# Layer B's first eight gate blocks as four block pairs ahead of the queries, gates kept in DRAM, scores and row minimum in one operation

## The chip, the cores and the metric

The kernel runs on one core of a Trainium2 chip. The metric is the device time of one execution in microseconds (us). TensorE (PE) multiplies matrices, VectorE (DVE) and ScalarE (ACT) work element by element, GpSimd (POOL) does some element work and issues transfers that add into their target, and SyncE (SP) issues nearly all other transfers, one after the other from one queue: a transfer that has to wait holds back all that stand behind it.

## The reference, cut to what matters

One step of a two-layer decoder on 576 tokens (512 of a prompt, 64 of eight samples), width 2048. Layer A is gated linear attention. Then one shared K and V is computed, and layer B is sliding-window attention with 32 heads, a sink per head and a distance penalty. Layer B is what the change touches:

```python
kv = rmsnorm(h, g_norm_kv) @ w_kv                   # shared K and V, 4 heads of 64
q, z = split(rmsnorm(h, g_norm_b) @ w_in, 2)        # w_in 2048 x 4096: 2048 columns q, 2048 columns z
s = (q . k) * HD ** -0.5 - slope * dist             # per head; -inf where not allowed
m = max(max(s), sink)
p = exp(s - m);  denom = sum(p) + exp(sink - m)
o = (p / denom) @ v
h = h + (o * silu(z)) @ w_out                       # silu(z): the gate
y = rmsnorm(h, g_final)
```

k and v of the last rows are outputs as well (`k_win_*`, `v_win_*`).

## The kernel before, in words

Activations lie with channels on the 128 partitions and the 576 tokens along the row. A weight matrix is taken in blocks of 128 output columns. Every fp32 product is done as three products of split numbers (high by high, high by low, low by high): a 512-wide piece of a weight block is loaded as `raw` (SP, L174), ACT rounds it to `wh` (L169), DVE subtracts to get `wl` (L170).

A **dense block** (`dense`) has 16 row tiles x 3 products x 2 token halves = 96 matmuls of 128 x 288 (L181). A **block pair** (`dense_pair`, used so far in the two output projections) computes two blocks with seven half-size products named A, P4, P5, B, P6, P7, C in that order, each of 8 row tiles x 3 = 24 matmuls (L251): 168 instead of 192. It needs sums of activations: `t1` in the second half of the x tiles, and `t2`, `t3`, `t4`, built by `sums` (L263, L267, L268) from the residual tiles `hp`. It also needs sums of weight quarters: the tiles `rs`, which SP loads (L231) and onto which a POOL transfer adds a second quarter from DRAM (L233). P5 uses the first such tile (`s1`), P7 the second (`s3`); the pair's plain quarters `w11`, `w22`, `w12` are `raw` tiles. Each stage opens its own memory pool over the space of the stage before, so its first tiles wait until all users of the old ones are done.

Layer B runs in this order. Four dense blocks for K and V, with the norm gain of K and V folded into the split of x. Keys are written to DRAM (`dk`, L928, L929), V stays in the tile `vm`; the window outputs are stored (L951 to L955). x is split again with layer B's gain (L96, L97). Then come 16 dense blocks q0 to q15 and 16 dense blocks z0 to z15. The attention runs as a background generator beside them: for each of 64 units (a head pair and 128 queries) and 16 sample units it inserts its few matmuls between those of the dense blocks. A unit of the prompt forms `slope*dist - score` with two DVE operations (L1028), takes the minimum with one (L1031), and goes on with exp, sum, reciprocal, scaling, transposes and the product with V. A sample unit does the same with three operations (L1092 twice, L1095) and one minimum (L1098). When a z block ends, its gate silu(z) is formed and multiplied onto the attention's result (L887 to L891); the background must have reached that head group by then.

The last six z blocks run in the pool of the output stage, with `sums` beside them; then follow one dense block of the output projection, six pairs and the last three blocks.

Of the kernel before, what the change touches and what calls it, by code (L numbers as in the profile page):

```python
# [37 lines left out]
def kernel(ctx: ExitStack, tc: tile.TileContext, A, O):  # L38
# [840 lines left out]

    units_done = [0]  # L880

    def z_phase(js):
        def ev(j):
            def f(p):
# [7 lines left out]
                if j < 8:  # L892
                    dma(dg2[j], hpt(j)[:, HT:NT])
            return f
        for j in js:
            yield from dense(A["wB"], KT + j, ev(j))

    with tc.tile_pool(name="ap", bufs=1) as ap:
# [13 lines left out]
        kw = ap.tile([128, 2, 256], F32, name="kw", tag="s", bufs=3)  # L912

        for k in range(KT):
            split_gain(k, hpt(k), GKV)

        def ev_k(m):
            def f(p):
                if m == 0:
                    finish(make_rstd(ssB[0], D, rstd, (0, 1)))  # L920
                t = st()
                vec.tensor_tensor(halves(t), p, rB2, ALU.mult)
                kh = ap.tile([128, NT], F32R, tag="stE", name=nm("kh"), bufs=2)
                kl = ap.tile([128, NT], F32R, tag="stO", name=nm("kl"), bufs=2)
                nc.scalar.copy(kh, t)
                vec.tensor_tensor(kl, t, f32(kh), ALU.subtract)
                for u in range(2):
                    dma(dk[2 * m + u, 0], f32(kh[u * 64:(u + 1) * 64, :]))  # L928
                    dma(dk[2 * m + u, 1], f32(kl[u * 64:(u + 1) * 64, :]))  # L929
                pt = bank(m)  # L930
                for i, c0 in enumerate((384, 448)):
                    nc.tensor.transpose(out=pt[:, i * 128:(i + 1) * 128], in_=t[:, c0:c0 + 128], identity=ident)
                nc.scalar.copy(kw[:, :, m * 128:(m + 1) * 128], pt[:, 0:256].rearrange("p (i f) -> p i f", i=2))
            return f

        def ev_v(m):
            def f(p):
                t = st()
                vec.tensor_tensor(halves(t), p, rB2, ALU.mult)
                pt = bank(2 + m)  # L940
                pt2 = bank(m)
                for i, c0 in enumerate((0, 128, 256, 384)):
                    nc.tensor.transpose(out=pt[:, i * 128:(i + 1) * 128], in_=t[:, c0:c0 + 128], identity=ident)
                nc.tensor.transpose(out=pt2[:, 0:128], in_=t[:, 448:576], identity=ident)
                nc.scalar.copy(vm[:, 0:4, m * 128:(m + 1) * 128], pt.rearrange("p (i f) -> p i f", i=4))
                nc.scalar.copy(vm[:, 4, m * 128:(m + 1) * 128], pt2[:, 0:128])
            return f

        run(chain(dense(A["wKV"], 0, ev_k(0)), dense(A["wKV"], 1, ev_k(1)),
                  dense(A["wKV"], 2, ev_v(0)), dense(A["wKV"], 3, ev_v(1))))  # L950
        dma(O["k_win_prompt"], kw[:, 0, :])  # L951
        dma(O["v_win_prompt"], vm[:, 3, :])
        for i in range(8):
            dma(O["k_win_sample"][i, 120:128], kw[64 + 8 * i:72 + 8 * i, 1, :])
            dma(O["v_win_sample"][i, 120:128], vm[64 + 8 * i:72 + 8 * i, 4, :])  # L955
        dma(O["k_win_sample"][:, 0:120], A["cache_k"][:, 8:128])
# [379 lines left out]
```

## Time and profile before

| | us |
|---|---|
| median of three runs | 1756.82 |
| the three runs | 1755.49, 1756.82, 1758.81 |
| the profiled execution | 1759.1 |
| its span in the profile | 1757.3 |
| PE busy in the span | 1728.8 |
| DVE busy | 1296.8 |
| ACT busy | 853.0 |

The profile is one execution. Its rows give start and duration of instructions or groups of them; a row of waits names the engine and line that waited and the one whose event ended the wait. The median lies 2.3 us below the profiled execution.

### The profile page before, as it was taken

What the parts mean: (1) busy time and instruction counts of PE and PEld (TensorE: products, weight loads), DVE (VectorE), ACT (ScalarE), POOL (GpSimd) and SP (SyncE); (2) the same over time, 40 slices, a digit from 0 to 9 for tenths busy, and PEclk for the clock granted to TensorE, in tenths of its full rate; (3) what the DMA queues carried; (4) which work ended last, traced back from release to release, by engine and by line L of the source; (5) the groups of instructions that cost most, each with busy time, mean ns of one, the idle gap of its engine ahead of it and who ended that gap; (6) DMA issues with size and microseconds to landing.
All of it is one profiled execution on the core that took longest, in us unless ns stands there. A gap on an engine that the chain in (4) does not pass through costs nothing.

```text
span 1757.3 us, 33753 instructions
## 1 busy us (share of the span) xinstructions
PE 1728.8 (98%) x12846; PEld 1709.1 (97%) x12846; DVE 1296.8 (74%) x2799; ACT 853.0 (49%) x1771; POOL 135.8 (8%) x216
## 2 busy tenths in 40 slices
PE   7999999999999999999999999999999999999996
PEld 7999999999999999999999999999999999999996
DVE  8566776777777777658777866888879885587784
ACT  7533334434434444435444655766666653364451
POOL 3000001001001000100111100100100000002210
PEclk9999999999999999999999999999999999999998
DMA  8246643565465444532677543343333225226643
GB/s 300 98 151 190 194 156 112 160 197 166 134 195 174 123 138 151 153 101 87 189 219 209 162 133 97 106 119 101 106 88 109 89 76 169 81 95 195 195 149 108
DMA packets 126690, 253.84 MB, mean 144 GB/s; under 512 B 22944, under 2 KB 52512, under 8 KB 126496
## 3 DMA queue, kind: packets, MB, share of 16 engines
q1 hardware_dynamic: 122784, 238.05, 42.2%
q0 software_dynamic: 3744, 13.63, 4.3%
q8 instruction: 101, 1.65, 0.4%
q14 instruction: 61, 0.50, 0.1%
HBM read 196.19 MB, written 44.83 MB: 137 GB/s over the span
## 4 chain that ended last, share of the span: by engine, by line
PE 91%; DVE 3%; issue 3%; DMA 2%; ACT 1%; SPq 0%; POOL 0%; POOLq 0%; DVEq 0%; ACTq 0%
PE pd L181 60%; PE pb L251 15%; PE pb L629 2%; PE pb L1041 1%; PE pb L715 1%; PE pb L1024 1%; PE pb L804 1%; PE pb L803 1%; PE pb L801 1%; PE pb L1023 1%; DVE wl L170 1%; PE pb L716 1%; PE pb L1051 1%; PE pb L1052 1%; DVE x L97 1%
## 5 line engine op out<-in xcount | busy, mean ns | idle before, releaser
L181 PE MATMUL pd<-x,wh 128*128 128x288 f32 x5568 | 1017.7, 299 | 10.1 <-ACT x L96 6.9
L181 PEld LDWEIGHTS pd<-x,wh 128*128 128x128 f32 x5568 | 837.0, 189 | 18.0 <-ACT x L96 6.9
L181 PE MATMUL pd<-x,wl 128*128 128x288 f32 x2784 | 614.1, 298 | 1.1 <-DVE wl L170 0.9
L169 ACT CAST wh<-raw 128x512 fp32r<-128x512 f32 x426 | 263.1, 618 | 403.7 <-PE pd L181 327.0
L181 PEld LDWEIGHTS pd<-x,wl 128*128 128x128 f32 x2784 | 454.1, 189 | 4.5 <-DVE wl L170 1.8
L170 DVE TENSOR_TENSOR wl<-raw,wh 128x512 fp32r<-128x512 f32 x426 | 306.2, 720 | 143.3 <-ACT wh L169 138.9
L251 PE MATMUL pb<-x,wh 128*128 128x288 f32 x832 | 166.7, 295 | 0.0
L251 PEld LDWEIGHTS pb<-x,wh 128*128 128x128 f32 x832 | 133.4, 188 | 0.0
L251 PE MATMUL pb<-t,wh 128*128 128x288 f32 x624 | 125.8, 296 | 0.7 <-ACT wh L169 0.6
L251 PE MATMUL pb<-x,wl 128*128 128x288 f32 x416 | 122.2, 295 | 0.0
L170 DVE TENSOR_TENSOR wl<-rs,wh 128x512 fp32r<-128x512 f32 x104 | 82.1, 793 | 32.2 <-ACT wh L169 30.0
L169 ACT CAST wh<-rs 128x512 fp32r<-128x512 f32 x104 | 64.0, 620 | 83.6 <-PE pb L251 76.6
L251 PEld LDWEIGHTS pb<-t,wh 128*128 128x128 f32 x624 | 100.2, 188 | 1.1 <-ACT wh L169 0.9
L251 PE MATMUL pb<-t,wl 128*128 128x288 f32 x312 | 92.4, 297 | 0.4 <-DVE wl L170 0.4
L251 PEld LDWEIGHTS pb<-x,wl 128*128 128x128 f32 x416 | 78.0, 188 | 0.0
L119 POOL TENSOR_TENSOR acc<-acc,st 128x576 f32<-128x576 f32 x46 | 70.1, 1523 | 83.1 <-ACT st L114 82.2
L117 POOL COPY acc<-st 128x576 f32<-128x576 f32 x7 | 6.3, 906 | 863.9 <-ACT st L114 775.9
L783 ACT CAST sh<-Si 128x512 fp32r<-128x512 f32 x64 | 39.7, 620 | 66.4 <-PE pb L803 43.6
L1033 ACT ACTIVATE s<-s,tiny 128x257 f32<-128x257 f32 (+1 forms) x128 | 60.9, 478 | 21.1 <-DVE tiny L1031 20.8
L114 ACT ACTIVATE st<-hp 128x576 f32<-128x576 f32 (+1 forms) x66 | 43.3, 663 | 40.8 <-DVE hp L1203 21.8
L251 PEld LDWEIGHTS pb<-t,wl 128*128 128x128 f32 x312 | 58.7, 188 | 0.8 <-DVE wl L170 0.8
L805 DVE SCALAR_TENSOR_TENSOR Si<-Si,dl,pb 128x512 f32<-128x512 f32 x64 | 47.5, 742 | 12.3 <-PE pb L801 11.7
(265 smaller groups left out, 2370.3 us busy)
## 6 DMA issues: line engine op xcount, KB each, us to landing
raw<-in_wA_dram SPq DMA_DIRECT2D x92, 512.0 KB
raw<-in_wB_dram SPq DMA_DIRECT2D x64, 512.0 KB
Si<-in_state_dram SPq DMA_DIRECT2D x64, 256.0 KB
out_gla_sample_dram<-Si SPq DMA_DIRECT2D x64, 256.0 KB
raw<-in_wOB_dram SPq DMA_DIRECT2D x26, 512.0 KB
raw<-in_wOA_dram SPq DMA_DIRECT2D x25, 512.0 KB
rs<-in_wOA_dram SPq DMA_DIRECT2D x14, 512.0 KB
rs<-in_wOA_dram POOLq DMA_DIRECT2D x14, 512.0 KB, 8.6
```

What stands on the lines that cost most here:

```text
L97: vec.scalar_tensor_tensor(t[:, 1, :], src, g, f32(t[:, 0, :]), ALU.mult, ALU.subtract)
L114: act(sq[:, lo:hi], src, AF.Square)
L119: self.eng.tensor_tensor(self.acc[:, lo:hi], self.acc[:, lo:hi], sq[:, lo:hi], ALU.add)
L169: nc.scalar.copy(wh, raw)
L170: vec.tensor_tensor(wl, raw, f32(wh), ALU.subtract)
L181: mm(p[:, a, :HT], w, x[:, part, a * HT:(a + 1) * HT], start=(k == 0 and w is wh and part == 0), stop=(k == KT - 1 and w is wl))
L251: mm(p, wt[:, kk, :], xpart(x, k, part), start=(opens and k == 0 and wt is wh and part == 0), stop=(k == 7 and wt is wl), skip_group_check ...
L629: mm(p[:, o:o + N], keys(li)[:, f * 128:(f + 1) * 128], queries(li)[:, f, :], start=(f == 0), stop=(f == 1))
L715: mm(p[:, sl], S[:, f, sl], qe[:, f, :], start=(f == 0), stop=False)
L783: nc.scalar.copy(sh, Si)
L805: vec.scalar_tensor_tensor(Si, Si, dl[:, f * 16 + i:f * 16 + i + 1], p, ALU.mult, ALU.add)
L1033: act(s[:, e, off:257], s[:, e, off:257], AF.Exp, scale=-1.0, bias=tiny[:, e:e + 1], accum_out=tiny[:, 2 + e:3 + e])
```

## The change

During the K/V blocks the residual `hp` is scaled in place by layer B's gain, and `sums_of_h` builds `t2`, `t3`, `t4` from it in the background. After the K/V blocks `vm` is stored to DRAM (`dvm`) and its pool is released; a new pool over that space holds the weight sums `rs` and two gate tiles. Four block pairs compute the z blocks 0 to 7; their gates go to DRAM (`dz`). Then the second halves of x are restored and the attention's pool opens, with `vm` loaded back. The z phase that is left covers blocks 8 to 15; each of its evictions also multiplies a stored gate onto block j - 8. In the attention, q is divided by minus the slope, so that one operation forms (score + dist) times slope and the minimum with the sink.

```diff
+    def pair_z(j):
+        def silu(j, rs):
+            th = st()
+            act(th, rs, AF.Tanh)
+            vec.scalar_tensor_tensor(rs, th, 1.0, rs, ALU.add, ALU.mult)
+            dma(dz[j], rs)
+        def f(n, p):
...
+            elif n == "P7":
+                vec.tensor_tensor(halves(r1), halves(r1), p.unsqueeze(1).broadcast_to([128, 2, HT]), ALU.subtract)
+                vec.scalar_tensor_tensor(r1, r1, 0.5, rstd, ALU.mult, ALU.mult)
+                silu(j + 1, r1)
+            elif n == "C":
+                vec.tensor_tensor(r0[:, HT:NT], p, u, ALU.subtract)
+                vec.scalar_tensor_tensor(r0[:, HT:NT], r0[:, HT:NT], 0.5, rstd[:, HT:NT], ALU.mult, ALU.mult)
+                silu(j, r0)
...
     def z_phase(js):
...
                 vec.tensor_tensor(hpt(j), hpt(j), rs, ALU.mult)
-                if j < 8:
-                    dma(dg2[j], hpt(j)[:, HT:NT])
+                i = j - 8
+                vec.tensor_tensor(hpt(i), hpt(i), early, ALU.mult)
+                dma(dg2[i], hpt(i)[:, HT:NT])
+            early = tpool[0].tile([128, NT], F32, tag="ld", name=nm("ld"), bufs=2)
+            dma(early, dz[j - 8])
...
+            def sums_of_h():
+                for g in range(4):
+                    for k in (2 * g, 2 * g + 1, 2 * g + 8, 2 * g + 9):
+                        act(hpt(k), hpt(k), AF.Copy, scale=vecs[:, GB + k:GB + k + 1])
+                        yield
+                    yield from sums_hp(g)
+            bgs.append([sums_of_h(), 1.1, 0.0])
...
+            dma(dvm, vm)
+            drain()
+        with tc.tile_pool(name="zq", bufs=1) as zq:
+            tpool[0] = zq
...
+            for j in range(0, 8, 2):
+                run(dense_pair(A["wB"], KT + j, pair_z(j)))
+    for k in range(8):
+        split_half(k, hpt(k)[:, HT:NT])
...
-            for e in range(2):
-                vec.scalar_tensor_tensor(s[:, e, off:256], distp[:, off:256], slope(2 * m + e),
-                                         p[:, e * 256 + off:(e + 1) * 256], ALU.mult, ALU.subtract)
-            tiny = tiny_tile()
-            vec.tensor_reduce(tiny[:, 0:2], s[:, :, off:257], AX.X, ALU.min)
+            tiny = tiny_tile()
+            for e in range(2):
+                i = 2 * m + e
+                vec.tensor_tensor_reduce(s[:, e, off:256], p[:, e * 256 + off:(e + 1) * 256], distp[:, off:256],
+                                         slope(i), sinkp[:, i:i + 1], ALU.add, ALU.min, tiny[:, e:e + 1])
...
-        run(z_phase(range(RS)))
+        run(z_phase(range(8, RS)))
```

The sample units are changed in the same way (three of the new operations each).

The first place is SP's queue behind the last K/V block. Before, the stores of `vm` (`out_v_win_*`) are followed by weights for the next q blocks (`raw`):

```order
L174 DMA raw_1712_12131<-in_wB_dram 128x1024
L174 DMA raw_1713_12133<-in_wB_dram 128x1024
L174 DMA raw_1749_12357<-in_wB_dram 128x1024
L952 DMA out_v_win_prompt_dram<-vm_11352 128x256
L955 DMA out_v_win_sample_dram<-vm_11352 8x256 x8
L174 DMA raw_1750_12359<-in_wB_dram 128x1024
L174 DMA raw_1785_12612<-in_wB_dram 128x1024
L976 DMA stE_1707_12120<-qh_1709_12122 64x576
```

In the changed kernel `raw_1707` and `raw_1709` are w22 and w12 of the first pair, `raw_1749` is w11 of the second, `rs_1708` and `rs_1710` are s1 and s3 of the first, `rs_1751` is s1 of the second:

```order
L231 DMA raw_1707_12084<-in_wB_dram 128x1024
L231 DMA raw_1709_12089<-in_wB_dram 128x1024
L231 DMA raw_1749_12346<-in_wB_dram 128x1024
L996 DMA out_v_win_prompt_dram<-vm_11345 128x256
L999 DMA out_v_win_sample_dram<-vm_11345 8x256 x8
L1003 DMA dvm_11338<-vm_11345 128x1280
L231 DMA rs_1708_12086<-in_wB_dram 128x1024
L231 DMA rs_1710_12091<-in_wB_dram 128x1024
L231 DMA rs_1751_12350<-in_wB_dram 128x1024
```

Behind the stores of `vm` there now stands the store `dvm`, and behind that the load of `rs_1708`, whose tile lies on the space that `vm` leaves.

The second place is TensorE at the same point. Before, the transposes of the last V block (`st` to `pb3` and `pb1`, L943, L944) stand inside block q0:

```order
L181 MATMUL pd_1695_12001<-x5_1684_11968,wh_1700_12034 128x288 x4
L181 MATMUL pd_1695_12001<-x5_1684_11968,wl_1701_12035 128x288
L943 MATMUL pb3_1677_11924<-c_ident_131,st_1676_11922 128x128 x4
L944 MATMUL pb1_1678_11925<-c_ident_131,st_1676_11922 128x128
L181 MATMUL pd_1695_12001<-x5_1684_11968,wl_1701_12035 128x288
L181 MATMUL pd_1695_12001<-x6_1685_11971,wh_1700_12034 128x288 x4
```

In the changed kernel they stand between product A (the last matmul of which is the first row here) and product P4:

```order
L251 MATMUL pb0_1711_12094<-x7_1697_12053,wl_1715_12112 128x288
L978 MATMUL pb3_1684_11976<-c_ident_131,st_1683_11974 128x128 x4
L979 MATMUL pb1_1685_11977<-c_ident_131,st_1683_11974 128x128
L251 MATMUL pb1_1719_12131<-t4_1631_11514,wh_1720_12132 128x288 x2
L251 MATMUL pb1_1719_12131<-t4_1631_11514,wl_1721_12133 128x288
```

and P4's last matmul is followed by P5, which takes `wh_1725`, cut from `rs_1708`:

```order
L251 MATMUL pb1_1719_12131<-t4_1631_11514,wh_1722_12148 128x288 x2
L251 MATMUL pb1_1719_12131<-t4_1631_11514,wl_1723_12149 128x288
L251 MATMUL pb2_1724_12165<-x0_1687_12012,wh_1725_12166 128x288 x2
L251 MATMUL pb2_1724_12165<-x0_1687_12012,wl_1726_12167 128x288
L251 MATMUL pb2_1724_12165<-x1_1688_12017,wh_1725_12166 128x288 x2
L251 MATMUL pb2_1724_12165<-x1_1688_12017,wl_1726_12167 128x288
```

The transposes moved from the middle of a dense block to the seam between two products of a pair, and P5 has only P4 ahead of it.

The third place is VectorE late in the z phase. Before, between the last weight split of z13 (`wl_2609`) and the first of z14 (`wl_2616`) there are three operations:

```order
L170 TENSOR_TENSOR wl_2609_18595<-raw_2600_18501,wh_2608_18594 128x512
L890 SCALAR_TENSOR_TENSOR st_2596_18492<-st_2597_18494,st_2596_18492 128x576
L891 TENSOR_TENSOR hp3_2258_15757<-hp3_2258_15757,st_2596_18492 128x576
L263 TENSOR_TENSOR st_2605_18547<-hp3_2258_15757,hp1_1900_13387 128x576
L170 TENSOR_TENSOR wl_2616_18637<-raw_2613_18632,wh_2615_18636 128x512
```

In the changed kernel there are nineteen operations between the last split of z14 (`wl_2695`) and the first of z15 (`wl_2703`), of which these are the last nine:

```order
L268 TENSOR_TENSOR t4_2637_18222<-st_2630_18144,t4_2637_18222 128x2x288
L268 TENSOR_TENSOR t2_2634_18178<-st_2662_18411,t2_2634_18178 128x2x288
L931 SCALAR_TENSOR_TENSOR st_2667_18489<-st_2668_18491,st_2667_18489 128x576
L263 TENSOR_TENSOR st_2662_18411<-st_2662_18411,hp2_2262_15694 128x576
L934 TENSOR_TENSOR hp1_2083_14541<-hp1_2083_14541,ld_2654_18360 128x576
L932 TENSOR_TENSOR hp3_2441_16871<-hp3_2441_16871,st_2667_18489 128x576
L928 SCALAR_TENSOR_TENSOR st_2681_18616<-pd_2670_18499,rstdB_11335 128x576
L934 TENSOR_TENSOR hp1_2083_14541<-hp1_2083_14541,ld_2669_18497 128x576
L268 TENSOR_TENSOR t4_2637_18222<-st_2662_18411,t4_2637_18222 128x2x288
L170 TENSOR_TENSOR wl_2703_18769<-raw_2700_18764,wh_2702_18768 128x512
```

The sums of the output stage (L263, L268) and the products with the stored gates (L934) have moved together to a place ahead of a weight split.

## Rows read from the trace of the kernel before

**Rows 1.** The page, part 1: busy time, share and count by engine.
```profile
PE 1728.8 (98%) x12846; PEld 1709.1 (97%) x12846; DVE 1296.8 (74%) x2799; ACT 853.0 (49%) x1771; POOL 135.8 (8%) x216
```

**Rows 2.** Waits of TensorE: who for whom, us in total, times, longest.
```profile
PE pb L932 <- DVE st L922: 1.8, 1, 1.8
...
PE pb L251 <- ACT wh L169: 0.6, 1, 0.6
...
PE pb L251 <- DVE wl L170: 0.4, 1, 0.4
```

**Rows 3.** Windows of 100 us: length, busy us by engine, clock, DMA share, GB/s.
```profile
1000.00:1100.00 100.00, 97.09 (x725) 96.45 (x725) 61.52 (x119) 53.01 (x115) 3.19 (x12) 0.98 0.43 126
...
1300.00:1400.00 100.00, 100.00 (x788) 100.00 (x787) 83.84 (x222) 66.33 (x194) 7.82 (x33) 1.00 0.33 100
```

**Rows 4.** Timeline of VectorE: start, us, line, evictions of dense blocks (q0, z7, z8, z9).
```profile
1060.57 0.76 DVE L967 SCALAR_TENSOR_TENSOR st<-pd,rstdB 128x576 f32<-128x576 f32 x1 [2.13 <-PE pd L181]
...
1451.54 0.76 DVE L887 SCALAR_TENSOR_TENSOR st<-pd,rstdB 128x576 f32<-128x576 f32 x1
...
1464.34 0.76 DVE L887 SCALAR_TENSOR_TENSOR st<-pd,rstdB 128x576 f32<-128x576 f32 x1 [2.07 <-PE pd L181]
...
1477.14 0.76 DVE L887 SCALAR_TENSOR_TENSOR st<-pd,rstdB 128x576 f32<-128x576 f32 x1 [2.07 <-PE pd L181]
```

**Rows 5.** Timeline of all engines after the last K/V block.
```profile
1052.33 0.59 ACT L945 COPY vm<-pb 128x512 f32<-128x512 f32 x1 [1.55 <-PE pb L943]
...
1052.81 0.27 ACT L946 COPY vm<-pb 128x128 f32<-128x128 f32 x1
...
1052.94 0.34 SPq L952 DMA_DIRECT2D out_v_win_prompt_dram<-vm  x1
...
1053.33 2.69 SPq L955 DMA_DIRECT2D out_v_win_sample_dram<-vm  x8
```

**Rows 6.** Waits of SyncE's queue.
```profile
SPq L772 <- DMA out_gla_sample_dram<-Si: 162.4, 57, 5.7
```

**Rows 7.** Timelines of SyncE and GpSimd where an output stage opens.
```profile
730.32 1.38 SPq L231 DMA_DIRECT2D rs<-in_wOA_dram  x3
...
737.23 1.06 POOL L233 DMA_DIRECT2D rs<-in_wOA_dram  x1 [23.84 <-DMA rs<-in_wOA_dram]
...
1452.47 0.43 SPq L231 DMA_DIRECT2D rs<-in_wOB_dram  x1
...
1460.04 0.92 POOL L233 DMA_DIRECT2D rs<-in_wOB_dram  x1 [27.56 <-DMA rs<-in_wOB_dram]
```

**Rows 8.** Tile rs: duration ns min/median/max; then its accumulating transfers.
```profile
L169 ACT CAST wh<-rs x104: 602/622/627, 835.4 to 1698.6; 128x512 fp32r<-128x512 f32 x104
...
L233 POOL DMA_DIRECT2D rs<-in_wOA_dram x14: 872/888/1064, 737.2 to 964.5; - x14
...
DMA to landing us min/median/max: 6.0/8.4/13.1
```

**Rows 9.** Windows after TensorE's wait of 1.8 us before 1015.82.
```profile
1016.00:1020.00 4.00, 4.00 (x20) 4.00 (x20) 1.73 (x3) 1.26 (x3) 0.00 (x0) 0.57 0.54 181
1020.00:1024.00 4.00, 4.00 (x33) 4.00 (x32) 2.11 (x3) 1.46 (x3) 0.00 (x0) 1.00 0.63 196
```

**Rows 10.** VectorE by line, 1050 to 1540: busy us, mean ns of one, idle before.
```profile
L1028 DVE SCALAR_TENSOR_TENSOR s<-distp,pb 128x256 f32<-128x256 f32 (+1 forms) x128 | 43.9, 382 | 10.9 <-PE pb L1024 10.4
...
L1031 DVE TENSOR_REDUCE tiny<-s 128x2 f32<-128x258 f32 (+1 forms) x64 | 39.3, 615 | 1.7
...
L1092 DVE SCALAR_TENSOR_TENSOR s<-dists,slops,pb 64x128 f32<-64x128 f32 x32 | 11.0, 345 | 3.5 <-PE pb L1085 3.2
...
L891 DVE TENSOR_TENSOR hp<-hp,st 128x576 f32<-128x576 f32 x14 | 10.6, 754 | 0.3
...
L1035 DVE RECIPROCAL tiny<-tiny 128x2 f32<-128x2 f32 x64 | 10.2, 159 | 11.5 <-ACT s L1033 11.1
...
L1098 DVE TENSOR_REDUCE tiny<-s 128x1 f32<-128x257 f32 x16 | 6.6, 410 | 0.1
...
L1095 DVE SCALAR_TENSOR_TENSOR s<-dists,slops,pb 128x16 f32<-128x16 f32 x16 | 3.7, 231 | 0.5
```

More of the change, by code (lines that the diff above doesn't have):

```diff
@@ L878, with zr @@
     dk = tc.dram_tile([4, 2, 64, NT], F32, name="dk")
+    dz = tc.dram_tile([8, 128, NT], F32, name="dz")
+    dvm = tc.dram_tile([128, 5, 256], F32, name="dvm")
     units_done = [0]
+    def pair_z(j):
+        tmp = []
+        def silu(j, rs):
[4 more added lines that the diff above has]
+        def f(n, p):
+            if n == "A":
+                tmp.append([st(), zr(), zr()])
+                nc.scalar.copy(tmp[0][0][:, 0:HT], p)
+                return
+            r1, r0 = tmp[0][1:]
+            u = tmp[0][0][:, 0:HT]
+            if n == "P4":
+                nc.scalar.copy(r1[:, 0:HT], p)
+            elif n == "P5":
+                nc.scalar.copy(r1[:, HT:NT], p)
+            elif n == "B":
+                vec.scalar_tensor_tensor(r0[:, 0:HT], p, 0.5, rstd[:, 0:HT], ALU.mult, ALU.mult)
+            elif n == "P6":
+                vec.tensor_tensor(u, p, u, ALU.subtract)
+                vec.tensor_tensor(halves(r1), u.unsqueeze(1).broadcast_to([128, 2, HT]), halves(r1), ALU.subtract)
+            elif n == "P7":
[6 more added lines that the diff above has]
+                silu(j, r0)
+        return f
+    def zr():
+        return tpool[0].tile([128, NT], F32, tag="zr", name=nm("zr"), bufs=2)
     def z_phase(js):
@@ L904 @@
         dma(slops, A["slops"])
+        qsc = ap.tile([128, 16], F32, name="qsc", tag="qsc")
+        dma(qsc, A["qsc"])
         sinkp = ap.tile([128, 32], F32, name="sinkp", tag="sinkp")
@@ L911 @@
         vm = ap.tile([128, 5, 256], F32, name="vm", tag="vm")
[L912 to L956, printed above, removed]
@@ L957 @@
-        dma(O["v_win_sample"][:, 0:120], A["cache_v"][:, 8:128])
-        for k in range(KT):
-            split_gain(k, hpt(k), GB)
+        dma(vm, dvm)
+        tpool[0] = ap
         stk = {}
@@ L966, in f @@
                 t = st()
-                vec.scalar_tensor_tensor(halves(t), p, 0.125, rB2, ALU.mult, ALU.mult)
+                vec.scalar_tensor_tensor(halves(t), p, qsc[:, m:m + 1], rB2, ALU.mult, ALU.mult)
                 E_ = ap.tile([128, NT], F32R, tag="stE", name=nm("stE"), bufs=2)
@@ L1261, in _consts @@
     hh = (s % 64) // 8
+    c["qsc"] = np.array([[-0.125 / slope(2 * m + p // 64) for m in range(16)] for p in range(128)], np.float32)
     c["slops"] = np.array([[slope(8 * j + h) for j in range(4)] for h in hh], np.float32)
```

71 lines of the change are left out of this document (65 added, 6 removed).

## The prediction

> **What bounds the kernel now.** I read the share of busy time by engine first: PE is busy for 1728.8 of 1757.3 us, DVE for 1296.8, ACT for 853.0 [rows 1]. So a change gains where it takes matmuls off PE, and loses where it makes PE wait. The list of PE's waits shows how little is left there: the longest in layer B is 1.8 us, and the thirteen pairs of the two output stages together waited 0.6 and 0.4 us for their weights [rows 2]. The windows tell the same of the attention: from 1300 to 1400 PE is busy all the time at full clock, while DVE has 83.84 us of work in 100 [rows 3]. The evictions of dense blocks give PE's step: z8 and z9, free of attention, end 12.80 us apart [rows 4], which for 96 matmuls is 0.1333 us each. From the end of q0 at 1060.57 to that of z7 at 1451.54 there are 23 blocks in 390.97 us [rows 4], 17.0 us each; less 12.8 each, the attention's own matmuls take 96.6 us of PE.
>
> **The gain.** A pair has 168 matmuls in place of 192. Four pairs save 4 x 24 x 0.1333 = 12.8 us, and since PE is the bound in this stage [rows 3], all of it counts as long as the pairs run without waits. Before, pairs did so [rows 2]; but there the weight sums had been loaded long before their use: the first loads went out at 730.32 and their first rounding came at 835.4 [rows 7, 8].
>
> **The first pair's weights.** This is the step on which I rest the forecast. The order of SP's queue shows the load of s1 right behind the stores of vm and the store dvm, and its tile lies where vm was, so that it cannot leave before dvm has landed. PE's order shows only product P4 between the moment when vm is complete and P5, which needs s1; no other matmul stands ready ahead of P5. From the end of the last copy to vm, which also lets P4 start, I add up:
> - the window stores: the copy ends at 1052.81 + 0.27 = 1053.08, the eighth sample store is issued at 1053.33 + 2.69 = 1056.02 [rows 5]: 3.0 us;
> - dvm from issue to landing. The trace has no such store. The nearest are the 256 KB state stores: SP waited 162.4 us in 57 times for them, 2.8 on the mean and 5.7 at most [rows 6]. dvm has 640 KB; I take 4.2, the middle between these two, and keep both ends;
> - the load of s1 until POOL can add to it: 737.23 - 730.32 = 6.9 and 1460.04 - 1452.47 = 7.6 us, both where a stage opens, at 730.32 with three such loads together, as here [rows 7]: 7.2 us;
> - the transfer that adds: 6.0 at least, 8.4 in the middle, 13.1 at most [rows 8]: 8.4 us;
> - the rounding on ACT: 0.6 us [rows 8].
>
> That is 3.0 + 4.2 + 7.2 + 8.4 + 0.6 = 23.4 us. P4 covers 24 x 0.1333 = 3.2 of them, and PE stands for 20.2 us. With the low ends it is 19.3 - 3.2 = 16.1, with the high ones 30.0 - 3.2 = 26.8.
>
> The 512 KB of a weight tile take 6.0 to 13.1 us in the accumulating transfer [rows 8]. The Trainium skill, page "SBUF — State Buffer", section "The DMA setup-cost knee (why "@ 1 MiB" ≠ asymptote)", fits a transfer as about 2 us plus its bytes over 436 GB/s; as an estimate that is 3.2 us for 512 KB and 3.5 for 640 KB. By it the chain would be 3.0 + 3.5 + 3.2 + 3.2 + 0.6 = 13.5, the stand 10.3 us and the whole sum below 2.1 in place of 12.0. The trace does not agree for the accumulating transfer, whose fastest took 6.0, so I keep to the rows.
>
> **What hangs on it.** After the 1.8 us wait before 1015.82 the granted clock was 0.57 over 4 us, and 20 matmuls ran where the next 4 us held 33 [rows 9]: 13 x 0.1333 = 1.7 us lost. A stand ten times as long ends in at least the same state; I add 1.7, between 0 and twice that.
>
> The five transposes of the last V block stood inside q0, where dense matmuls ran on during the copies. Now P4 takes the bank of one of them and stands directly behind. The copies ended at 1053.08, begun at 1052.33 [rows 5]; I add 0.9 for the copies and the step to the first of them.
>
> **Costed at nothing.** Scaling hp in place (16 ACT operations), the sums of activations and the splits of x lie beside the four K/V blocks, 51 us of PE, in a stretch where DVE has 61.5 and ACT 53.0 us of work in 100 [rows 3]; their price is 0, and 2 us if the last splits are late for product A. The gates' evictions, silu and the stores dz lie beside the next pair. Reloading vm, the distance tables and the keys waits for the last gate's store, but q0 and most of q1 run before the first score needs them; 12.8 + 9 us cover that. If the cover fails, attention starts late and more of it is left at the end, worth at most the 4.6 us that it adds to one block.
>
> **The scores.** The removed DVE operations sum to 43.9 + 39.3 + 11.0 + 6.6 + 3.7 = 104.5 us [rows 10]. In their place come 176 of the new kind (two for each of 64 units, three for each of 16), each with a second small instruction that hands over the minimum. The trace has no such operation. From below it costs what the matching two-input operation costs (43.9 + 11.0 + 3.7 = 58.6); from above each also bears a minimum of the old kind, 104.5 in all, and 176 x 0.159 (the small reciprocal [rows 10]) = 28.0 for the hand-over. I take 58.6 + 28.0 = 86.6, a saving of 18 us on DVE; the ends are a saving of 46 and a loss of 28. On the path none of it counts while PE is full: the attention now lies beside 21 blocks instead of 23, so PE has 12.8 + 96.6 / 21 = 17.4 us a block, and DVE, at 0.84 of 17.0 us before, has 14.3 x 23 / 21 = 15.6 at most. Price 0.
>
> **The end of the z phase.** Eight of the sixteen z blocks were free of attention; now about two are. The order of DVE shows 19 operations in one piece between the splits of z14 and z15, at 0.754 us [rows 10] some 14.3 us against the 12.8 of the block that covers them; a second such piece follows ahead of the first output block. I add 2 us for both, between 0 and 5.
>
> **Sum.** -12.8 + 20.2 + 1.7 + 0.9 + 2.0 = +12.0 us on the profiled execution's 1759.1, that is 1771.1. The median lies 2.3 below that execution, so the forecast is 1769. Its own range is from -12.8 + 16.1 + 0.9 = +4.2 (1761) to -12.8 + 26.8 + 3.4 + 0.9 + 5 + 2 = +25.3 (1782).
>
> **The rivals.**
> First, not slower: s1 comes early enough, the 12.8 us are gained. The mechanism would be that the tile of s1 is free sooner than the order suggests, so that its load and its adding transfer run beside the last K/V blocks, as they did in both output stages [rows 7, 8]. It decides when s1 is complete within P4, that is 23.4 - 3.2 = 20.2 us earlier than I expect. Against it stands that dvm reads vm, which is complete only behind the last K/V block. The time: -12.8 + 0.9 + 2.0 = -9.9, so 1747.
>
> Second, quick transfers: the chain is as I say, but little else is on the queues at that moment (the output stages loaded weights and residuals beside), and each piece takes its low end or less. Then the sum is +4 or below, 1756 to 1761. It decides where store, load and adding transfer together stay under 2.8 + 6.9 + 6.0 = 15.7 us. By the fit of the Trainium skill's page "SBUF — State Buffer" the time would be 1759.
>
> Third, the attention becomes bound by DVE. For it speaks that the new operation is unknown; DVE without the old ones has 15.6 - 104.5 / 21 = 10.6 us in a block of 17.4, so 6.8 us are left for 8.4 of the new, 0.8 us each with the hand-over. Below that, nothing; at 1.0 us each, 21 x 8.4 x 0.2 = 35 us on top, about 1804. Against it: a 128 x 256 operation would need twice the time of any two-input one here.
>
> **How the numbers follow.** The forecast has 0.70, the first rival 0.13, the second 0.12, the third 0.05. A measurement of this kernel can tell 0.2% from no change, 3.5 us: faster than 1753.3 is the first rival and a little of the second, 0.14; within are the lower half of the second, 0.07; slower is the rest, 0.79. The range of 8 in 10 leaves out the first rival below and the third above: 1756 to 1782.
>
> **What would show it.** In the changed kernel's trace: PE waiting in P5 for the rounding of s1, once, by some 20 us, and in no other pair; the load of s1 issued 7 us behind the last copy to vm; pairs 22.4 us apart after that; a granted clock below 1 behind the wait; attention blocks near 17.4 us with PE full; a wait of PE on a weight split at z15 or the first output block. I am wrong if that wait is under 10 us, or if PE idles in the attention.

## The result, and the profile after

| | before | changed |
|---|---|---|
| median, us | 1757.82 (4 runs) | 1785.28 (4 runs) |
| lowest to highest | 1755.49 to 1761.44 | 1782.19 to 1790.76 |
| the profiled execution | 1759.1 | 1784.65 |
| its span | 1757.3 | 1782.9 |

The ratio is 1.0156 with a 95% interval of 1.0140 to 1.0172: slower, as forecast. But from profile to profile it is +25.6 us where the sum had +12.0, and 1785.28 lies above the range, which ended at 1782. The direction and the largest term were right; a term that was put at 2 us measured about 17.

Part 1 of the page of the changed kernel answers to [rows 1]:

```profile
PE 1723.7 (97%) x12750; PEld 1701.2 (95%) x12750; DVE 1326.0 (74%) x2991; ACT 890.0 (50%) x1851; POOL 140.9 (8%) x224
```

PE has 96 matmuls less than before and is busy 5.1 us less, but the kernel takes 25.6 us longer: what was lost is idle time and time at a lower clock. The waits of PE from 1030 to 1600 us of the changed kernel (us in total, times, longest) answer to [rows 2]:

```profile
PE pb L251 <- ACT wh L169: 18.0, 2, 15.9
PE pd L181 <- DVE st L928: 6.9, 1, 6.9
PE pb L1106 <- DMA raw<-in_wB_dram: 4.1, 1, 4.1
PE pd L181 <- DVE wl L170: 2.0, 4, 1.1
PE pb L251 <- DVE wl L170: 1.4, 2, 0.9
PE pb L251 <- ACT vm L981: 0.7, 1, 0.7
```

Where before the longest was 1.8 us, there are now three long ones, in three places: the first pair's P5 (L251), the first scores (L1106), and a dense block late in the z phase (L181 for an eviction, L928). To see what each place cost, cut the run at two events that both kernels have: the eviction of q0 on VectorE [rows 4, for before], and the first addition of an output pair on GpSimd. VectorE and GpSimd of the changed kernel:

```profile
1165.73 0.82 DVE L1050 SCALAR_TENSOR_TENSOR st<-pd,qsc,rstdB 128x576 f32<-128x576 f32 x1 [2.08 <-PE pd L181]
...
1614.98 1.43 POOL L119 TENSOR_TENSOR acc<-acc,st 128x576 f32<-128x576 f32 x1 [0.99 <-ACT st L114]
```

GpSimd of the kernel before, the same addition:

```profile
1589.39 1.44 POOL L119 TENSOR_TENSOR acc<-acc,st 128x576 f32<-128x576 f32 x1 [0.32 <-ACT st L114]
```

- Up to q0 the changed kernel is 1165.73 - 1060.57 = 105.16 us later. Four pairs without waits are 4 x 168 x 0.1333 = 89.6, so 15.6 us too many.
- From q0 to the addition it needs 1614.98 - 1165.73 = 449.25 us, before 1589.39 - 1060.57 = 528.82. Eight dense blocks of 12.80 us have gone from this part (102.4), which would leave 426.4: 22.8 us too many.
- -12.8 + 15.6 + 22.8 = +25.6, the whole difference.

That the pairs themselves take the 22.4 us each that is used here shows in VectorE's timeline, where the same step of the second and the third pair stands 22.3 us apart:

```profile
1101.89 0.46 DVE L908 TENSOR_TENSOR st<-pb,st 128x288 f32<-128x288 f32 x1 [0.34 <-PE pb L251]
...
1124.21 0.46 DVE L908 TENSOR_TENSOR st<-pb,st 128x288 f32<-128x288 f32 x1 [0.34 <-PE pb L251]
```

So 15.6 of the loss lies ahead of the end of q0, in the first pair, where 22.8 was forecast (20.2 + 1.7 + 0.9), and 22.8 behind q0, where 2.0 was.

**The first pair.** The chain that ended last, from 1045 to 1092 of the changed kernel (start, us, what), shows the forecast's steps in their order:

```profile
1047.13 0.03 ACT vm L981
1047.15 3.62 DMA out_v_win_prompt_dram<-vm
...
1051.11 2.95 DMA dvm<-vm
...
1054.59 5.06 DMA rs<-in_wB_dram
...
1059.69 6.33 DMA rs<-in_wB_dram
...
1066.04 0.63 ACT wh L169
...
1066.71 25.32 PE pb L251 x166
```

From the copy of `vm` to P5 it takes 19.5 us: stores 4.0 (forecast 3.0), the store `dvm` 3.1 (4.2), the load of s1 5.5 (7.2), the transfer that adds 6.35 (8.4), the rounding 0.6. PE's wait in it is the 15.9 us of the list above, and the clock behind it is in the first of these windows:

```profile
1066.00:1074.00 8.00, 7.29 (x32) 7.07 (x33) 4.33 (x6) 3.40 (x7) 0.00 (x0) 0.55 0.67 162
1074.00:1082.00 8.00, 8.00 (x62) 8.00 (x62) 6.32 (x10) 3.44 (x7) 0.00 (x0) 1.00 0.38 131
1178.00:1182.00 4.00, 4.00 (x22) 4.00 (x23) 2.86 (x14) 1.69 (x7) 0.09 (x1) 0.62 0.99 347
...
1543.00:1549.00 6.00, 5.86 (x29) 5.89 (x30) 4.87 (x7) 3.05 (x6) 2.22 (x3) 0.61 1.02 295
```

The columns are those of [rows 3]; the last two windows belong to the two other places. After the wait the granted clock is 0.55 of full speed, most of the 8 us at the lower level (1.2 GHz); in the 7.29 busy us PE ran 32 matmuls where 7.29 / 0.129 = 56 fit at the pace of the next window, 24 x 0.1333 = 3.2 us lost. 15.9 + 0.7 + 3.2 = 19.8. Against that, the last V block's eviction comes 3.7 us sooner than before (VectorE, 1043.70 against 1047.43), because the 1.8 us wait of [rows 2] and the low clock of [rows 9] are gone there. 19.8 - 3.7 = 16.1, the 15.6 to within half a microsecond.

**The start of the attention.** The first score waits 4.1 us, and 4 x (1 - 0.62) = 1.5 us go with the clock behind it: 5.6 us. SP's queue shows what stands ahead of it:

```profile
1155.96 0.33 SPq L892 DMA_DIRECT2D dz<-zr  x1
1160.09 0.33 SPq L1027 DMA_DIRECT2D distp<-in_distp_dram  x1
...
1162.84 0.43 SPq L1042 DMA_DIRECT2D vm<-dvm  x1
...
1171.09 0.60 SPq L1060 DMA_DIRECT2D stO<-ql  x1
```

The tables, `vm` and the keys go out only when the last gate's store has landed, 4.1 us later; q's rows follow at 1169 to 1172. SP's queue was not what held these rows back at the last: SP stood still from 1168.1 to 1169.3, until ScalarE had rounded q (1168.59 to 1169.26), and on ScalarE that stands behind the split of the reloaded `vm` (1167.34), before which it had waited 4.4 us for a load. In the kernel before, the first of q's rows left 1.8 us after q0's eviction began, here 3.5 us. The list of waits names a weight load for the first score, but GpSimd, which takes the same rows, shows what came at that moment; the score started at 1177.87:

```profile
1177.85 0.24 POOL L1095 CAST qs<-stO 128x64 fp32r<-128x64 f32 x1 [0.49 <-DMA stO<-ql]
```

The DMA engines were 0.98 busy from 1175 to 1178, while the rows were under way.

**The end of the z phase.** The first score of the kernel before waited too, for 1.1 us, so 4.5 of the 5.6 are new, and 22.8 - 4.5 = 18.3 us are left. VectorE of the changed kernel, the stretch of the 6.9 us wait and behind it:

```profile
1535.39 1.03 DVE L1209 TENSOR_TENSOR hp<-hp,t 64x64 f32<-64x64 f32 x4
1536.83 0.69 DVE L170 TENSOR_TENSOR wl<-raw,wh 128x512 fp32r<-128x512 f32 x1 [0.42 <-ACT wh L169]
1537.44 0.75 DVE L268 TENSOR_TENSOR t<-st,t 128x576 fp32r<-128x576 f32 x1
1538.23 0.76 DVE L263 TENSOR_TENSOR st<-st,hp 128x576 f32<-128x576 f32 x1
1539.36 1.63 DVE L934 TENSOR_TENSOR hp<-hp,ld 128x576 f32<-128x576 f32 x2 [0.38 <-DMA ld<-dz]
...
1542.24 0.75 DVE L928 SCALAR_TENSOR_TENSOR st<-pd,rstdB 128x576 f32<-128x576 f32 x1
...
1551.16 0.76 DVE L934 TENSOR_TENSOR hp<-hp,ld 128x576 f32<-128x576 f32 x1 [3.19 <-DMA ld<-dz]
...
1557.09 0.76 DVE L934 TENSOR_TENSOR hp<-hp,ld 128x576 f32<-128x576 f32 x1 [3.83 <-DMA ld<-dz]
```

and SP in the same stretch:

```profile
1536.56 0.80 SPq L937 DMA_DIRECT2D ld<-dz  x2
...
1541.70 0.64 SPq L937 DMA_DIRECT2D ld<-dz  x1
```

The attention's last operations (L1209) run from 1535.39 to 1536.4. Only then is its pool free, and only then do the loads of the stored gates for the pool of the output stage go out; the first sums (L268), whose tiles lie in that pool, start only then as well. The eviction of z12 (L928), for which PE waits, stands on VectorE behind all of this: two products with stored gates (L934) and four operations of the sums (L263, L268). For the gates' loads alone VectorE waits only 0.4 us here. The next two gates are waited for by VectorE itself, 3.2 and 3.8 us, while its backlog grows. That backlog is paid after 1580, where VectorE is busy 19.96 of 20 us and PE 15.98:

```profile
1500.00:1550.00 50.00, 43.08 (x321) 42.88 (x320) 37.32 (x110) 27.36 (x75) 4.19 (x12) 0.93 0.37 116
...
1580.00:1600.00 20.00, 15.98 (x111) 14.82 (x111) 19.96 (x34) 7.95 (x16) 0.00 (x0) 0.97 0.16 54
```

In microseconds: PE's waits between 1540 and 1600 are 6.9 for the eviction and 5.6 in seven shorter ones; the clock costs 2.3 in the window at 1543, 0.6 at 1580 and 2.8 at 1600 (0.72 over 10 us). That is 18.2, less the 1.1 that PE idled at the same place before: 17.1 of the 18.3 that were to be found; 1.2 us are not placed.

**The scores.** VectorE by line, 1160 to 1540 of the changed kernel (busy us, mean ns of one, idle before), answers to [rows 10]:

```profile
L1113 DVE CUSTOM_DVE_ANT_0 s<-pb,distp,sinkp 128x256 f32<-128x256 f32 (+1 forms) x128 | 52.4, 447 | 18.6 <-PE pb L1107 14.2 <-POOL s L1109 3.1 <-PE pb L1124 0.8
L1176 DVE CUSTOM_DVE_ANT_0 s<-pb,dists,sinks 64x128 f32<-64x128 f32 x32 | 13.1, 409 | 5.1 <-POOL s L1172 3.2 <-PE pb L1168 1.5
L1113 DVE DVE_READ_ACCUMULATOR2_ANT tiny<- 128x1 f32 x128 | 10.5, 82 | 0.0
L1180 DVE CUSTOM_DVE_ANT_0 s<-pb,dists,tiny 128x16 f32<-128x16 f32 x16 | 4.6, 291 | 0.6
L1176 DVE DVE_READ_ACCUMULATOR2_ANT tiny<- 64x1 f32 x32 | 2.6, 80 | 0.0
L1180 DVE DVE_READ_ACCUMULATOR2_ANT tiny<- 128x1 f32 x16 | 1.3, 83 | 0.0
```

Together 84.5 us, forecast 86.6, in place of 104.5.

### The profile page after: what moved, and what is told of

Same layout as the page of the kernel before. It is cut to its first block, busy times and chain, and to the rows that moved or that the text cites. A ratio compares the mean times of both kernels' runs of the same rounds, so it can differ in the third digit from the quotient of the medians.

```text
span 1782.9 us, 34051 instructions
## 1 busy us (share of the span) xinstructions
PE 1723.7 (97%) x12750; PEld 1701.2 (95%) x12750; DVE 1326.0 (74%) x2991; ACT 890.0 (50%) x1851; POOL 140.9 (8%) x224
## 4 chain that ended last, share of the span: by engine, by line
PE 88%; DMA 5%; DVE 4%; issue 2%; ACT 1%; SPq 0%; POOL 0%; POOLq 0%; DVEq 0%; ACTq 0%
PE pd L181 53%; PE pb L251 20%; PE pb L629 2%; PE pb L1124 1%; PE pb L715 1%; DMA ld<-dz 1%; DMA hp<-in_xT_dram 1%; PE pb L1107 1%; DVE wl L170 1%; PE pb L804 1%; PE pb L803 1%; PE pb L1106 1%; PE pb L801 1%; PE pb L716 1%; PE pb L1135 1%
## 5 line engine op out<-in xcount | busy, mean ns | idle before, releaser
L181 PE MATMUL pd<-x,wh 128*128 128x288 f32 x5056 | 929.5, 299 | 17.1 <-ACT x L96 7.0
L181 PEld LDWEIGHTS pd<-x,wh 128*128 128x128 f32 x5056 | 761.1, 189 | 25.0 <-issue 9.6
L181 PE MATMUL pd<-x,wl 128*128 128x288 f32 x2528 | 556.7, 298 | 3.6 <-DVE wl L170 3.4
L181 PEld LDWEIGHTS pd<-x,wl 128*128 128x128 f32 x2528 | 412.1, 189 | 7.9 <-DVE wl L170 5.2
L251 PE MATMUL pb<-x,wh 128*128 128x288 f32 x1088 | 220.7, 297 | 15.9 <-ACT wh L169 15.9
L251 PEld LDWEIGHTS pb<-x,wh 128*128 128x128 f32 x1088 | 176.9, 190 | 16.1 <-ACT wh L169 16.1
L251 PE MATMUL pb<-t,wh 128*128 128x288 f32 x816 | 166.2, 298 | 2.9 <-ACT wh L169 2.1
L251 PE MATMUL pb<-x,wl 128*128 128x288 f32 x544 | 161.4, 298 | 1.6 <-DVE wl L170 1.6
L251 PEld LDWEIGHTS pb<-t,wh 128*128 128x128 f32 x816 | 132.4, 190 | 3.3 <-ACT wh L169 2.4
L251 PE MATMUL pb<-t,wl 128*128 128x288 f32 x408 | 122.2, 300 | 1.0 <-DVE wl L170 0.8
L251 PEld LDWEIGHTS pb<-x,wl 128*128 128x128 f32 x544 | 103.2, 190 | 2.5 <-DVE wl L170 2.5
L251 PEld LDWEIGHTS pb<-t,wl 128*128 128x128 f32 x408 | 77.6, 190 | 2.0 <-DVE wl L170 2.0
L1116 ACT ACTIVATE s<-s,tiny 128x257 f32<-128x257 f32 (+1 forms) x128 | 61.0, 479 | 19.2 <-DVE tiny L1113 18.3
L1113 DVE CUSTOM_DVE_ANT_0 s<-pb,distp,sinkp 128x256 f32<-128x256 f32 (+1 forms) x128 | 52.4, 447 | 18.6 <-PE pb L1107 14.2
```

The source lines that it names most:

```text
L181: mm(p[:, a, :HT], w, x[:, part, a * HT:(a + 1) * HT], start=(k == 0 and w is wh and part == 0), stop=(k == KT - 1 and w is wl))
L251: mm(p, wt[:, kk, :], xpart(x, k, part), start=(opens and k == 0 and wt is wh and part == 0), stop=(k == 7 and wt is wl), skip_group_check ...
L1113: vec.tensor_tensor_reduce(s[:, e, off:256], p[:, e * 256 + off:(e + 1) * 256], distp[:, off:256], slope(i), sinkp[:, i:i + 1], ALU.add, A ...
L1116: act(s[:, e, off:257], s[:, e, off:257], AF.Exp, scale=-1.0, bias=tiny[:, e:e + 1], accum_out=tiny[:, 2 + e:3 + e])
```

## The experiments

Two theories were set against each other. H, the handover of pools: the loss comes from first tiles of a pool that wait for all users of the pool before, in the three places. D, density: eight z blocks fewer leave too little room for the attention and for VectorE's work. All experiments but the one on the scores alone start from the changed kernel; times are medians, with the ratio to the kernel before on the same chip and its 95% interval. Differences to the changed kernel compare medians of different chips, on which the kernel before took 1757.8 to 1758.6 us.

**The stored gates early.** All eight gates are loaded and multiplied in z8 and z9, in the attention's pool; in the changed kernel six of them stand in z10 to z15.

```diff
-                i = j - 8
+            for i in range(4 * (j - 8), 4 * (j - 7)) if j < RS else ():
+                early = tpool[0].tile([128, NT], F32, tag="ld", name=nm("ld"), bufs=2)
+                dma(early, dz[i])
                 vec.tensor_tensor(hpt(i), hpt(i), early, ALU.mult)
                 dma(dg2[i], hpt(i)[:, HT:NT])
-            early = tpool[0].tile([128, NT], F32, tag="ld", name=nm("ld"), bufs=2)
-            dma(early, dz[j - 8])
```

> The changed kernel, with all eight stored gates loaded and multiplied in blocks z8 and z9, in the attention's pool, instead of one in each of z8 to z15. Theory H (handover): at the end of the z phase the eviction of z12 stands on VectorE behind products with stored gates, which can only be loaded when the attention's pool is given up; so the wait of 6.9 us and a good part of the 17.8 us lost there goes: 8 to 14 us faster than the changed kernel, 1771 to 1777. Rival D (density): VectorE simply has too much work beside too few free blocks; the eight operations move into an even fuller stretch, and the time stays within 3 us of 1785.

1774.39 us, ratio 1.0087 [1.0070, 1.0104]: 10.9 below the changed kernel. z12's eviction on VectorE no longer stands behind a gate that comes late:

```profile
1524.37 0.75 DVE L928 SCALAR_TENSOR_TENSOR st<-pd,rstdB 128x576 f32<-128x576 f32 x1
...
1541.77 0.49 DVE L1209 TENSOR_TENSOR hp<-hp,t 64x64 f32<-64x64 f32 x2 [0.31 <-ACT hp L1208]
```

It ran while the attention was still going (its end is the second row), and PE's wait for an eviction fell from 6.9 to 0.3 us, although the attention itself ended 6 us later than in the changed kernel. So most of the 17 us hung on what stands behind the handover of the attention's pool; D had expected no gain. The run takes two things out of that stretch at once, VectorE's waits for the loads (0.4 + 3.2 + 3.8 = 7.4 us) and six products (6 x 0.75 = 4.5 us of work), and z12's eviction came to stand ahead of the sums; what each was worth it does not show. Some stays: from 1570 to 1604 PE is still busy only 29.72 of 34, with VectorE busy 31.45 and the longest wait of PE, 2.3 us, for one of its splits (L285). That part looks like D's.

**Product B ahead of P5.** Twenty-four more matmuls before s1 is needed.

```diff
...
-                run(dense_pair(A["wB"], KT + j, pair_z(j)))
+                run(dense_pair(A["wB"], KT + j, pair_z(j), ("A", "P4", "B", "P5", "P6", "P7", "C")))
```

> The changed kernel, with product B ahead of P5 in the four gate pairs. Theory H: the chain from the last copy of V to the rounded s1 has a length of its own, 19 us; 24 more matmuls beside it shorten TensorE's wait from 15.9 by 3.2 to 12.7 us, and the kernel by about 3 (1782). Rival: what starts the chain or ends it hangs on TensorE's own order (a bank, the split of x), and the wait stays near 16 (1785).

1783.18 us, ratio 1.0141 [1.0122, 1.0159], 2.1 less; the interval overlaps that of the changed kernel (1.0140 to 1.0172), so the time alone decides nothing. In the profile the wait shrank by 3.5, about the 3.2 us of product B:

```profile
1068.24 0.85 PE L252 MATMUL pb<-x,wh 128*128 128x288 f32 x2 [12.36 <-ACT wh L169]
```

The chain to s1 has a length of its own; what runs ahead of P5 only covers part of it.

**Two dense blocks ahead of three pairs.** 25.6 us of matmuls that need no weight sums.

```diff
...
+            for j in range(2):
+                run(dense(A["wB"], KT + j, first_z(j)))
...
-            for j in range(0, 8, 2):
+            for j in range(2, 8, 2):
                 run(dense_pair(A["wB"], KT + j, pair_z(j)))
```

> The changed kernel, with z0 and z1 as dense blocks between the K/V blocks and three pairs (z2 to z7): 25.6 us of matmuls that need no weight sum stand ahead of the first pair. Theory H: the wait for s1 goes, with the clock loss behind it and the wait at P4 (15.9 + 3.2 + 0.7 = 19.8), and one pair's gain (3.2) is given up: 16.6 us faster than the changed kernel, about 1769. Rival: the first pair's weights hang on something later than V (the state of the pool, GpSimd's queue), and over 8 us of wait remain: 1776 or more.

1777.10 us, ratio 1.0109 [1.0092, 1.0126]: 8.2 less, half of what was expected, and near the rival's time. But the rival's reason does not hold: the wait for s1 is gone (1.5 us is the longest on a rounding), but 3.2 go with one pair less, and a new wait came in, on VectorE first and then on PE:

```profile
1079.51 0.76 DVE L1025 TENSOR_TENSOR st<-hp 128x576 f32<-128x576 f32 x1 [4.05 <-DMA dz<-st]
```

```profile
1081.29 0.61 PE L251 MATMUL pb<-x,wh 128*128 128x288 f32 x1 [5.42 <-DVE x L285]
```

The operation at 1079.51, a step of the splits for the pairs, needs a buffer out of which a gate is still being stored. The expectation had not counted that a store holds the buffer until it has landed.

**The new scores alone**, in the kernel before.

```diff
...
-            for e in range(2):
-                vec.scalar_tensor_tensor(s[:, e, off:256], distp[:, off:256], slope(2 * m + e),
-                                         p[:, e * 256 + off:(e + 1) * 256], ALU.mult, ALU.subtract)
             tiny = tiny_tile()
-            vec.tensor_reduce(tiny[:, 0:2], s[:, :, off:257], AX.X, ALU.min)
+            for e in range(2):
+                i = 2 * m + e
+                vec.tensor_tensor_reduce(s[:, e, off:256], p[:, e * 256 + off:(e + 1) * 256], distp[:, off:256],
+                                         slope(i), sinkp[:, i:i + 1], ALU.add, ALU.min, tiny[:, e:e + 1])
...
```

Not shown of the diff are the division of q by minus the slope and the sample units.

> The kernel before, with the new scores alone (one operation that also keeps the minimum), no pairs of gates. Theory H: VectorE has some 20 us less work, but TensorE is full there, so the time stays within 3 us of before (1755 to 1761). Rival D: the new operation lengthens a unit's chain or loads VectorE, and the kernel is 5 us or more slower; or the attention did hang on VectorE, and it is 5 or more faster.

1758.09 against 1758.57 us, ratio 0.9999 [0.9989, 1.0008]: no change, as the price 0 said. Yet the attention ended 28 us sooner, VectorE's last row of it here and then in the kernel before:

```profile
1423.15 0.49 DVE L1128 TENSOR_TENSOR hp<-hp,t 64x64 f32<-64x64 f32 x2 [0.31 <-ACT hp L1127]
```

```profile
1450.98 0.49 DVE L1126 TENSOR_TENSOR hp<-hp,t 64x64 f32<-64x64 f32 x2 [0.31 <-ACT hp L1125]
```

**The changed kernel with the old scores**, the other half of that question; its diff is the one above turned round.

> The changed kernel with the scores of the kernel before (two operations and a minimum in each unit), pairs of gates as they are. Theory H: VectorE has 20 us more to do, over 21 blocks in which TensorE is full; within 3 us of the changed kernel, 1782 to 1788. Rival D: the new scores are what lets VectorE keep up beside fewer blocks; without them the attention ends later and the loss at the end of the z phase grows: 1790 or more.

1796.02 us, ratio 1.0212 [1.0197, 1.0226]: 10.7 above the changed kernel. Here H's expectation failed and D was right. PE's wait for z12's eviction grew from 6.9 to 8.4 us, and two windows show the stretch behind the attention:

```profile
1500.00:1550.00 50.00, 43.30 (x302) 40.69 (x300) 40.75 (x122) 33.50 (x108) 2.83 (x14) 0.87 0.13 45
1550.00:1580.00 30.00, 23.39 (x162) 23.40 (x163) 21.78 (x32) 9.86 (x17) 2.70 (x3) 0.82 0.82 231
```

The attention ends at 1549.8 instead of 1536.4, so the pool is handed over later still (the stored gates' loads go out at 1549.95 instead of 1536.56), and fewer matmuls are left to run beside the output stage's preparation. In these two pairs of runs the new scores are worth nothing where eight z blocks follow the attention, and about 10 us where hardly any do. H and D are thus no opposites: the density sets when the attention ends, and the handover makes that end count.

**s1 ahead of `vm`.** `vm` gets a pool of its own on top of the keys' pool, so that the weight sums' tiles lie over memory that is free before the V blocks end.

```diff
...
-            vm = kp.tile([128, 5, 256], F32, name="vm", tag="vm")
+            kp.tile([128, 256], F32, name="pad", tag="pad")
...
+            vp.append(vstack.enter_context(tc.tile_pool(name="vp", bufs=1)))
+            vp.append(vp[0].tile([128, 5, 256], F32, name="vm", tag="vm"))
...
+            vstack.close()
+        with tc.tile_pool(name="zq", bufs=1) as zq, tc.tile_pool(name="zg", bufs=1) as zg:
             tpool[0] = zq
+            zpool.append(zg)
```

> The changed kernel with V in a small pool of its own above the tiles of the keys, and the weight sums rs in the space of the keys' tiles alone, so that s1 and s3 of the first pair no longer wait for the stores of V; all operations are the same. Theory H: s1 is loaded during the V blocks, the waits at P5 and P4 and the clock loss behind them go: 19 us faster than the changed kernel, about 1765. Rival: the adding transfer or the stores of V only move the wait to s3, to the next quarters or to the gates' tiles, and 8 us or more of it remain: 1773 or more.

1768.04 us, ratio 1.0060 [1.0046, 1.0073]: 17 less than the changed kernel. SP's queue of this kernel:

```profile
1034.11 1.50 SPq L231 DMA_DIRECT2D rs<-in_wB_dram  x3
...
1051.97 0.34 SPq L1004 DMA_DIRECT2D out_v_win_prompt_dram<-vm  x1
...
1055.26 0.35 SPq L1011 DMA_DIRECT2D dvm<-vm  x1
```

The load of s1 now goes out 18 us before the stores of `vm`, and P5's wait of 15.9 us is gone. That is the forecast's main step, shown by taking its cause away; at P4 PE now waits 1.3 us instead of 0.7.

**Both together**: the last diff and that of the early gates.

> The same, with the stored gates multiplied in z8 and z9 as in the run of that alone (which took 10.9 us off). Theory H: the two places are apart and the gains add up: 1785 - 19 - 11 = 1755, that is 3 us faster than the kernel before. Rival: with TensorE earlier at the start of the attention, what was hidden behind its wait (the loads of keys, V and tables) comes out, and a third or more of one gain is lost: 1761 or more, slower than before.

1757.90 us, ratio 0.9997 [0.9987, 1.0008]. Of the sum of 17.2 and 10.9, 27.4 us came: the two losses are separate.

**The attention's first unit later.** On top of both, its first unit lets four more steps of the generator pass, so that q's rows have landed.

```diff
-                    for _ in range(2):
+                    for _ in range(2 if u[0] else 6):
                         yield
```

> The same again, with the attention's first unit placed four half steps later among the matmuls of q1 and q2. Theory H: the wait of about 3 to 4 us for the first stacked queries, with the clock loss of 1.7 behind it, goes, since q's matmuls stand ahead of it: 4 us faster than the run without it, about 1751. Rival: the wait is for transfers that come later by as much, or the attention's end is later by as much at the output stage: no gain (1755).

1753.86 us, ratio 0.9979 [0.9970, 0.9988], 4.0 less again; PE's wait at the first scores went from 3.2 to 1.0 us. So the start of the attention was a loss of its own. What is left lies at the end: from 1560 to 1570 PE is busy 7.70 us and VectorE 10.00.

**A higher rate for the attention**, 1.15 in place of 0.95, on top of that.

```diff
-        bgs.append([attention(), 0.95, 0.0])
+        bgs.append([attention(), 1.15, 0.0])
```

> The version of att_later with the attention's rate at 1.15 instead of 0.95 steps for each half step of a dense block. Theory H: the attention is paced by the queries' blocks and by its own chain on VectorE and ScalarE, not by the rate; it ends at most a block earlier, and the time is 1751 to 1755. Rival: the rate paces it; it ends two or more blocks earlier, the loss at the end goes, and the time is 1748 or less.

1756.88 us, ratio 0.9994 [0.9985, 1.0004]: no gain, and above the 1751 to 1755 that H had given. The attention ended at 1517.5 instead of 1519.3. From 1200 to 1500 PE was busy 296.70 us, with the lower rate 299.72, and from 1550 to 1580 26.62 against 27.01. The rate is not what holds the attention's end; a higher one only makes PE wait inside it.

**Three pairs**, z6 and z7 dense again, on top of the later first unit; the six stored gates are multiplied in z8 and z9.

```diff
...
-            for j in range(0, 8, 2):
+            for j in range(0, 6, 2):
                 run(dense_pair(A["wB"], KT + j, pair_z(j)))
...
-        run(z_phase(range(8, RS)))
+        run(z_phase(range(6, RS)))
```

> The version of att_later with three pairs (z0 to z5); z6 and z7 are dense blocks at the start of the z phase. TensorE gets 3.2 us more of matmuls, and two more blocks stand behind the attention. Theory H: what is left at the end of the z phase in att_later (about 5 us of waits and 3 us of clock between 1500 and 1580) comes from the attention ending at 1519 with only two free blocks behind it; with four it shrinks to 2 or less, and the time is 1754 + 3.2 - 6 = 1751. Rival: the loss at the end is the output stage's own splits and sums, and it stays: 1757.

1752.90 us against 1758.02, ratio 0.9965 [0.9953, 0.9977]: 5.1 us under the kernel before, and the lowest ratio of all. Its windows at the end of the z phase:

```profile
1500.00:1550.00 50.00, 50.00 (x377) 50.00 (x376) 37.97 (x56) 26.72 (x46) 2.71 (x3) 1.00 0.48 142
1550.00:1580.00 30.00, 28.89 (x213) 28.21 (x212) 25.98 (x44) 14.06 (x26) 1.01 (x1) 1.00 0.39 129
```

PE is full there but for 1.1 us, as much as it idled in the kernel before, and the clock stays at 1.00. A pair less costs 3.2 us of matmuls, and two more dense blocks between the attention and the output stage give that back; against four pairs the difference (0.9965 to 0.9979) is within the two intervals.

## Why the prediction was wrong, point by point

- **The gain, 12.8.** It came: the pairs behind the first stand 22.3 us apart, two dense blocks take 25.6, and three mended pairs show 5.1 of their 3 x 3.2 = 9.6 us in the time.
- **The first pair's weights, 20.2 (16.1 to 26.8).** Mechanism right, measured 15.9, just under the low end; s1 ahead of `vm` removes it. The three transfers behind the stores were near or below their low ends: `dvm` 3.1 (low end 2.8), the load 5.5 (6.9), the one that adds 6.35 (6.0); the stores alone were longer. That was the second rival's condition: 3.1 + 5.5 + 6.35 = 15.0, under its 15.7. By this step alone the second rival, and not the forecast, was right. Its reason fits as well, though no run tests it: the DMA engines were 0.69 and 0.85 busy during this load and this adding transfer, and 0.90 and 1.00 where the first output stage opened (730 to 746 us of the kernel before). The 2.8 and 5.7 us for `dvm` were SP's waits for other stores, not times to landing; the store itself took 2.95.
- **The clock, 1.7 (0 to 3.4).** 3.2, near the upper end.
- **The wait of P4, 0.9.** 0.7.
- **K and V, 0.** The first pair's stage even gained 3.7, since `rstdB` no longer comes late: in the chain of the kernel before, a transfer (`cv`, 5.4 us from 1002.13) stands ahead of `rstdB` and the 1.8 us wait; in the changed kernel PE is busy 55.00 of the 55 us from 990 to 1045, before 53.17.
- **"On the path none of it counts while PE is full ... Price 0"**, the scores. True for the attention: from 1190 to 1500 PE is busy 310.00 of 310 us. True for the scores alone. Not for what the attention's end sets off: with the old scores the changed kernel takes 10.7 us longer. No term was wrong by this, since both edits were made, but the reason given was too narrow.
- **"Reloading vm, the distance tables and the keys ... 12.8 + 9 us cover that".** Failed: 0 forecast, 5.6 measured, 4.5 more than before; 4 came back with the later first unit. The store of the last gate took 4.1 us first, and on ScalarE the rounding of q stands behind the split of the reloaded `vm`. The price named for a failed cover, 4.6 us, was near, but it was to be paid at the attention's end.
- **"The end of the z phase ... I add 2 us for both, between 0 and 5".** This is the step that failed: about 17. It counted nineteen operations by their busy time, 14.3 against a block's 12.8. But these operations need a pool that is free only when the attention ends: the sums write into it, and the stored gates must first be loaded into it. In VectorE's order z12's eviction stood behind them, and PE waited 6.9 us for it at the start of z14, ahead of the place that the forecast had looked at. With the gates taken out of that pool 10.9 us came back. The waits that the forecast did name, on weights at the last z blocks and the first output block, came too, and at 5.6 us were longer than its upper bound of 5; the rest is clock, 2.3 + 0.6 + 2.8.

The sum of the first pair's terms was 7.2 too high and that behind q0 20.8 too low, so the error of 13.6 is smaller than the mistake. Nearly all of its signs came as well (one wait at the first s1, its load 7 us behind the last copy to `vm`, pairs 22.3 us apart, PE full in the attention), so they could not have warned of the total. That the total was too low has one cause above all: the handover of `vm`'s pool was followed through in detail, while the same rule at the attention's pool, with the same kind of load behind it, was passed over as a count of busy time.

What stays open: how the 10.9 us of the early gates divide between loads, work and order, what of the 4 us that PE still idled there is VectorE's load alone, and why three pairs realise 5.1 of 9.6 us. In the three pairs' profile 3.3 us are lost between q0 and the first addition of the output stage, by the same count as above (1581.31 - 1125.98 = 455.33, against 528.82 - 6 x 12.8 = 452.02); waits of 1.7, 1.3 and 1.2 us remain (in the attention, at P4 and at the first scores).

## What to carry to other kernels

When a change moves work from behind a stage to ahead of it, look at both ends: what it takes away from the far end was cover for the next handover. At each place where one pool takes over another's memory, write down the last reader or transfer of the old one, then the first load into the new one, and then what stands behind that load's consumer on an engine that works in order; do it for every handover, and not only for the one the change adds. Work that is free while an engine has slack may be what sets the end of a background job, so its price has to be asked for again when the slack behind that end is spent.

## What the runs showed of the hardware that was not expected

- The combined operation (difference, scaling and minimum) costs 479 ns at 128 x 256 and 348 at 128 x 128 (447 on the mean), plus 82 ns for the small instruction that hands over the minimum; the old form cost 382 ns twice and 615 ns once, on the mean, for a unit of the prompt [rows 10].
- The clock's price behind a wait grew much less than the wait: 3.2 us after 15.9 us, 2.3 after 6.9, 1.5 after 4.1, and 1.7 after the 1.8 us of the kernel before [rows 9]. Each is what the windows above hold.
- Transfers that add into their target took 5.5 us at least, 8.5 in the middle and 12.9 at most in the changed kernel, much as in [rows 8]; the 640 KB store `dvm` landed in 2.95 us, where SP had waited 2.8 us on the mean for a store of 256 KB in [rows 6].
